# Down-projection weights loaded two neighbouring rows per partition, with the activations transposed by every second column

## The chip, the cores and the metric

The kernel runs on one core of one Trainium2 chip. The metric is the device time of one execution in microseconds (us). Three runs of the kernel before gave 1525.69, 1526.43 and 1526.97 us; the median is 1526.43 us.

## The reference, cut to what matters

The program is one decoder layer on 512 tokens of width 1024: a state-space mixer and a pooling mixer, a layer norm, a mixture of 32 experts of which every token uses 4, and a second layer norm. The change lies in the experts. One expert block, with its inputs `xb` (tokens by 1024) and the expert's number `e`, is

```python
g = xb @ w_gate[e] + b_gate[e]
u = xb @ w_up[e] + b_up[e]
g = jnp.minimum(g, SWIGLU_LIMIT)
u = jnp.clip(u, -SWIGLU_LIMIT, SWIGLU_LIMIT)
glu = g * jax.nn.sigmoid(SWIGLU_ALPHA * g)
return ((u + 1.0) * glu) @ w_down[e] + b_down[e]
```

All three weights of an expert are 1024 x 1024 float32, 4 MB each. The results of a token's four experts are added with the router's weights. All weights of all 32 experts (384 MB) are read from HBM once.

## The kernel before

A front part (the mixers, the first norm, the router, the gate of the per-layer inputs) fills the first 410 us. Then come the experts, one after the other in the fixed order `ORD`, and a short tail with the last norm. An expert has 64, 96 or 128 slots for tokens (`CAP`, only experts 2 and 3 have 128); its slots are worked on in blocks of 32 (`NB` = 4 blocks at most).

**Loads.** Every weight matrix is loaded in four quarters of 256 rows of the contraction, 1 MB each, into a ring of 16 buffers of 128 partitions x 2 x 1024 float32 (`raw_tile`, `RAWS`). `raw_load` (L1212 to L1216) issues them from SyncE in the order gate 0 to 3, up 0 to 3, down 0 to 3, and `do_load` issues the load 16 places ahead as soon as the matmuls of the present one are in the program. For gate and up, partition p of quarter q holds the rows 8p + 2q and 8p + 2q + 1, which are neighbours in HBM (8 KB in one piece, 32 KB from the piece of the next partition). For down, partition p holds the rows 256q + p and 256q + 128 + p (two pieces of 4 KB, 512 KB apart; the pieces of neighbouring partitions are neighbours in HBM).

**Matmuls.** `mm_tile` (L1117 to L1127) multiplies one quarter: for each block of 32 slots and each of the two rows of a partition, four matmuls of 32 stationary columns and 256 moving columns, one for each quarter of the output columns, which lie in four strips of 32 output partitions. Two instructions stand in the trace for each of them, so a quarter of an expert with 64 slots shows 32 instructions, with 96 slots 48, with 128 slots 64. The kernel's loop goes over positions i in `ORD`: in position i come gate and up of expert i, then down of expert i - 1.

**Between them.** The result of gate and up leaves `u2` with 32 x 4 partitions (strip j, slot) and, for block b, 256 columns; the element at strip j and column c is hidden unit 256j + c. `h_T` (L1138 to L1142) turns it over for the down matmuls by TensorE transposes of 128 x 128 (`u2` is the stationary operand, `ident` the moving one) and a copy on ScalarE into `ht`. A transpose takes 128 columns that lie next to each other: the first takes the columns 0 to 127 of the block, the second 128 to 255, which fits rows p and 128 + p of a quarter. `h_T_rows` (L1144 to L1151) does the same for the last expert, whose down matmuls go through `mm_rows`. Beside the weights, GpSimd issues for every position the indirect transfers that add the results to the output rows (L1160, four 256-column pieces at most) and gather the inputs of a later expert (L1016).

A loop for overflowing experts (at the end of the file) uses the same helpers.

Of the kernel before, what the change touches and what calls it, by code (L numbers as in the profile page):

```python
# [37 lines left out]
NB = 4  # L38
# [30 lines left out]
def _layer(top, tc, nc, x, xT, pT, ssm, ssm_d, log_step, w_in, w_val, w_glg, w_pg, pscale, w_pp,  # L69
# [5 lines left out]
    TE = nc.tensor  # L75
# [11 lines left out]
    def tps():  # L87
        return psum.tile([128, 512], F32, tag="tp", name="tp", bufs=2)
# [30 lines left out]
    ident = keep.tile([128, 128], F32, name="ident")  # L119
# [55 lines left out]
    def new():  # L175
        slot[0] += 1
        return sm[:, slot[0] - 1]
# [64 lines left out]
    kq, r = new(), new()  # L242
# [97 lines left out]
    for q4 in range(4):  # L340
        pt = tps()
# [248 lines left out]
    for slot in range(24):  # L590
# [4 lines left out]
        g_, n_ = ((up_g, 1) if slot < 4 else (gb_g, 1) if slot < 12 else (pp_g, 2) if slot < 16 else (ga_g, 1))  # L595
# [6 lines left out]
    for kk in range(4):  # L602
        pt = tps()
# [380 lines left out]
    def raw_tile(dt_=F32):  # L984
        pool, tag, bufs = ring[rn[0] % RAWS]
        rn[0] += 1
        return pool.tile([128, 2, D], dt_, tag=tag, name="eraw", bufs=bufs)
# [3 lines left out]
    for n in range(len(ring)):  # L991
        r = raw_tile()
# [145 lines left out]
    def h_T(u2, ht, g_, n_=2):  # L1138
        pt = tps()
        for i in range(2 * n_):  # L1140
            TE.transpose(pt[:, i * 128:(i + 1) * 128], u2[:, (4 * g_ + i) * 128:(4 * g_ + i + 1) * 128], ident)  # L1141
        S.copy(ht[:, 2 * g_:2 * g_ + n_], pt[:, :256 * n_].rearrange("p (b u c) -> p b u c", b=n_, u=2))  # L1142

    def h_T_rows(u2, ht, g_, n_):  # L1144
        pt = tps()
        for i in range(2 * n_):
            TE.transpose(pt[:, i * 128:(i + 1) * 128], u2[:, (4 * g_ + i) * 128:(4 * g_ + i + 1) * 128], ident)
        for i in range(n_):
            b = 2 * g_ + i
            S.copy(ht.rearrange("p (j u) c -> p u j c", u=2)[:, :, :, b * 32:(b + 1) * 32],  # L1150
                   pt[:, i * 256:(i + 1) * 256].rearrange("p (u j s) -> p u j s", u=2, j=4))  # L1151
# [16 lines left out]
    def g_min(pg, w_=512):  # L1168
        g_ = mz.tile([128, 512], F32, tag="g", name="g", bufs=2)
        ts(g_[:, :w_], pg[:, :w_], LIMIT, OP.min)  # L1170
        return g_
# [14 lines left out]
    def u2_tile():  # L1186
        return mz.tile([128, D], F32, tag="u2", name="u2", bufs=2)
# [23 lines left out]

    def raw_load(src, q_, down):  # L1212
        r = raw_tile()
        v = src.rearrange("(k p) c -> p k c", p=128) if down else src.rearrange("(p k) c -> p k c", k=8)
        nc.sync.dma_start(r, v[:, 2 * q_:2 * q_ + 2])
        return r  # L1216

    seq = []
# [9 lines left out]
    def do_load(n):  # L1228
        if n < len(seq) and n not in raws:
            i, m_, q_ = seq[n]  # L1230
            c = ORD[i - (m_ == 2)]
            w_ = (w_gate, w_up, w_down)[m_]
            if c < 2:
                src = w_[c]
            else:
                if c not in RG:
                    RG[c] = nc.sync.value_load(eid[0:1, c:c + 1], min_val=0, max_val=(E - 1) * D)
                src = w_.rearrange("e k c -> (e k) c")[bass.ds(RG[c], D), :]
            raws[n] = raw_load(src, q_, m_ == 2)
# [5 lines left out]
    def hooks(i, s):  # L1245
# [4 lines left out]
        if s == 0:  # L1250
            if p_ is not None:
                HT[p_] = h_tile() if i < E else x_tile()
                for g_ in banks(p_):
                    if i < E:
                        h_T(U2[p_], HT[p_], g_, min(2, nb_of(p_) - 2 * g_))
                    else:
                        h_T_rows(U2[p_], HT[p_], g_, min(2, nb_of(p_) - 2 * g_))
            if c is not None:
                PG[c], PU[c] = ([acc() for _ in banks(c)] for _ in range(2))
                if i > 0:  # L1260
                    bias(0, c)(PG[c])
                    bias(1, c)(PU[c])
            if nx is not None:
                X[nx] = x_tile()
                for q_ in range(2):
                    half_T(xgs[(i + 1) % 2], X[nx], q_, CAP[nx], (S.copy, V.tensor_copy)[q_])
                SL[nx] = sel_e(nx)
            if i + 2 < E:
                gather(xgs[i % 2], ls[:, ORD[i + 2]], CAP[ORD[i + 2]])
# [98 lines left out]
    with tc.manual_schedule():  # L1368
# [11 lines left out]
        for i in range(E + 1):  # L1380
            for s in range(12):
# [6 lines left out]
                if here:  # L1388
                    _, m_, q_ = seq[n]
                    w_ = raws.pop(n)  # L1390
                    if m_ == 2:
                        c = ORD[i - 1]
# [7 lines left out]
                    else:  # L1400
                        c = ORD[i]
# [27 lines left out]
    with tc.For_i(0, nb_, 1) as it:  # L1429
# [36 lines left out]
        for m_ in range(2):  # L1466
            os = [acc(), acc()]
            for q_ in range(4):
                mm_tile(os, xt_, raw_load(wv[m_], q_, False), q_, NB, pre=bias_v(m_))
            pp.append(os)  # L1470
        u2 = u2_tile()
        for n0 in range(2):
            g_ = g_min(pp[0][n0])
            tt(g_, g_, g_sig(g_), OP.mult)
            glu(u2, n0, u_clip(pp[1][n0]), g_)
        for g_ in range(2):
            h_T(u2, ht_, g_)
        os = [sacc(), sacc()]
        for q_ in range(4):
            mm_tile(os, ht_, raw_load(wv[2], q_, True), q_, NB, True, True)  # L1480
# [47 lines left out]
```

## Time and profile before

| | us |
|---|---|
| median of three runs | 1526.43 |
| the profiled execution | 1529.48 |
| its span, first to last instruction | 1527.8 |
| TensorE matmuls busy | 1359.0 (89%) |
| VectorE / GpSimd / ScalarE busy | 438.5 / 286.4 / 245.8 |
| bytes read from HBM | 453 MB |

Slices of the page show the DMA engines nearly idle for stretches of the front part and fully busy from about 420 us to about 1460 us, at 372 to 408 GB/s. A load is a DMA issued by SyncE ("SPq"); it is split over 16 DMA engines and has landed when the slowest of them is done. In a row of a timeline the first two numbers are the start and the length of a run of like instructions; "x32" is their count; the brackets hold the idle time ahead and what ended it.

### The profile page before, as it was taken

What the parts mean: (1) busy time and instruction counts of PE and PEld (TensorE: products, weight loads), DVE (VectorE), ACT (ScalarE), POOL (GpSimd) and SP (SyncE); (2) the same over time, 40 slices, a digit from 0 to 9 for tenths busy, and PEclk for the clock granted to TensorE, in tenths of its full rate; (3) what the DMA queues carried; (4) which work ended last, traced back from release to release, by engine and by line L of the source; (5) the groups of instructions that cost most, each with busy time, mean ns of one, the idle gap of its engine ahead of it and who ended that gap; (6) DMA issues with size and microseconds to landing.
All of it is one profiled execution on the core that took longest, in us unless ns stands there. A gap on an engine that the chain in (4) does not pass through costs nothing.

```text
span 1527.8 us, 41208 instructions
## 1 busy us (share of the span) xinstructions
PE 1359.0 (89%) x18454; PEld 876.3 (57%) x18454; DVE 438.5 (29%) x940; ACT 245.8 (16%) x436; POOL 286.4 (19%) x293
## 2 busy tenths in 40 slices
PE   6779999999699999997989889989898899799993
PEld 6658887767566665554545445545454455456651
DVE  3986747577311111110101011111110111111105
ACT  2434334242100010000100000000100000000011
POOL 0294310003401121111112111111121111110132
PEclk9889999999899999999999999999999999999997
DMA  4412325731699999999999999999999999999963
GB/s 154 134 53 72 99 86 194 222 116 46 219 401 389 398 389 372 390 397 394 393 388 387 386 377 384 392 388 395 383 393 382 381 381 395 391 384 405 408 210 139
DMA packets 124164, 468.58 MB, mean 307 GB/s; under 512 B 19757, under 2 KB 44785, under 8 KB 91216
## 3 DMA queue, kind: packets, MB, share of 16 engines
q1 hardware_dynamic: 107248, 446.12, 75.8%
q0 software_dynamic: 16736, 19.79, 6.0%
q8 instruction: 146, 2.39, 0.6%
q14 instruction: 34, 0.28, 0.1%
HBM read 453.23 MB, written 17.80 MB: 308 GB/s over the span
## 4 chain that ended last, share of the span: by engine, by line
DMA 48%; PE 39%; DVE 5%; issue 4%; POOL 3%; ACT 0%; SPq 0%; DVEq 0%; ACTq 0%; POOLq 0%
DMA eraw<-in_w_down_dram 22%; DMA eraw<-in_w_up_dram 14%; PE acc L1125 14%; PE ss L1125 9%; DMA eraw<-in_w_gate_dram 8%; PE acc L116 3%; PE acc L117 3%; PE acc L115 3%; DMA lsb<-in_log_step_dram 2%; POOL lst L817 1%; PE acc L1132 1%; PE tp L1141 1%; PE acc L1208 1%; PE tp L1009 1%; DMA raw<-in_w_out_dram 1%
## 5 line engine op out<-in xcount | busy, mean ns | idle before, releaser
L1125 PE MATMUL acc<-eraw,xt 128*32 128x256 f32 x10880 | 619.2, 386 | 67.8 <-DMA eraw<-in_w_up_dram 62.3
L1125 PEld LDWEIGHTS acc<-eraw,xt 128*32 128x32 f32 x10880 | 350.2, 111 | 324.5 <-DMA eraw<-in_w_up_dram 90.2
L1125 PE MATMUL ss<-eraw,ht 128*32 128x256 f32 x5312 | 298.3, 380 | 20.4 <-DMA eraw<-in_w_down_dram 20.4
L1160 POOL DMA_INDIRECT acc_d<-y,ix x83 | 129.6, 1561 | 880.2 <-ACT y L1194 864.3
L1125 PEld LDWEIGHTS ss<-eraw,ht 128*32 128x32 f32 x5312 | 171.5, 110 | 143.1 <-DMA eraw<-in_w_down_dram 33.7
L1142 ACT COPY ht<-tp 128x512 f32<-128x512 f32 (+1 forms) x50 | 23.9, 516 | 659.3 <-PE tp L1141 659.3
L183 DVE TENSOR_SCALAR u<-acc 128x512 f32<-128x512 f32 (+1 forms) x51 | 30.6, 600 | 301.9 <-PE acc L1125 293.3
L181 DVE TENSOR_SCALAR g<-acc 128x512 f32<-128x512 f32 (+1 forms) x51 | 30.7, 603 | 288.9 <-PE acc L1125 278.4
L1010 DVE COPY xt<-tp 128x384 f32<-128x384 f32 (+2 forms) x32 | 16.4, 512 | 312.4 <-PE tp L1009 312.3
L115 PE MATMUL acc<-ahi,hi 128*128 128x512 f32 x160 | 64.5, 403 | 15.2 <-DVE sm L191 15.2
L1175 ACT ACTIVATE s<-g 128x512 f32<-128x512 f32 (+1 forms) x51 | 27.9, 559 | 284.6 <-DVE g L181 284.6
L104 DVE TENSOR_TENSOR lo<-raw,hi 128x1024 fp32r<-128x1024 f32 (+1 forms) x52 | 63.1, 1216 | 28.2 <-ACT hi L103 27.8
L103 ACT CAST hi<-raw 128x1024 fp32r<-128x1024 f32 (+1 forms) x53 | 54.9, 1036 | 72.4 <-PE acc L116 48.8
L117 PE MATMUL acc<-ahi,lo 128*128 128x512 f32 x160 | 64.0, 400 | 0.0
L116 PE MATMUL acc<-alo,hi 128*128 128x512 f32 x160 | 63.7, 398 | 0.0
L115 PEld LDWEIGHTS acc<-ahi,hi 128*128 128x128 f32 x160 | 31.0, 194 | 21.7 <-ACT hi L103 15.5
L1016 POOL DMA_INDIRECT xg<-hd,ls x32 | 32.5, 1017 | 33.3 <-PE tp L1009 23.9
L116 PEld LDWEIGHTS acc<-alo,hi 128*128 128x128 f32 x160 | 31.0, 194 | 6.3
L117 PEld LDWEIGHTS acc<-ahi,lo 128*128 128x128 f32 x160 | 30.7, 192 | 6.6
L1194 ACT ACTIVATE y<-ss,ls 128x256 f32<-128x256 f32 x83 | 33.9, 482 | 0.0
L187 DVE TENSOR_TENSOR g<-g,s 128x512 f32<-128x512 f32 (+1 forms) x51 | 29.2, 601 | 13.1 <-ACT s L1175 13.1
L191 DVE SCALAR_TENSOR_TENSOR u<-u,g 128x512 f32<-128x512 f32 (+1 forms) x51 | 30.8, 603 | 1.7
(404 smaller groups left out, 1291.6 us busy)
## 6 DMA issues: line engine op xcount, KB each, us to landing
eraw<-in_w_gate_dram SPq DMA_DIRECT2D x128, 1024.0 KB
eraw<-in_w_up_dram SPq DMA_DIRECT2D x128, 1024.0 KB
eraw<-in_w_down_dram SPq DMA_DIRECT2D x128, 1024.0 KB
raw<-in_w_in_dram SPq DMA_DIRECT2D x23, 512.0 KB
raw<-in_w_out_dram SPq DMA_DIRECT2D x8, 512.0 KB
raw<-in_w_ple_gate_dram SPq DMA_DIRECT2D x8, 512.0 KB
raw<-in_w_pool_proj_dram SPq DMA_DIRECT2D x4, 512.0 KB
raw<-in_w_glu_val_dram SPq DMA_DIRECT2D x4, 512.0 KB
```

Source lines behind the costliest of these rows:

```text
L103: S.copy(h, v)
L104: (lo_eng or V).tensor_tensor(l, v, h.bitcast(F32), op=OP.subtract)
L115: TE.matmul(o, lhsT=lh, rhs=rh, start=start, stop=False)
L116: TE.matmul(o, lhsT=lh, rhs=rl, start=False, stop=False)
L117: TE.matmul(o, lhsT=ll, rhs=rh, start=False, stop=stop)
L181: V.tensor_scalar(o, i, a, None, op0=op)
L183: V.tensor_scalar(o, i, a, b, op0=op, op1=op1)
L191: V.scalar_tensor_tensor(o, a, s, b, op0=op0, op1=op1)
L1016: P.indirect_dma_start(out=xg[:n_], out_offset=None, in_=hd, in_offset=bass.IndirectOffsetOnAxis(ap=lst_[:n_, 0:1], axis=0), bounds_check= ...
L1125: TE.matmul(os[b // 2][j * 32:(j + 1) * 32, b % 2 * 256:b % 2 * 256 + 256], lhsT=x_, rhs=w_[:, kk, j * 256:(j + 1) * 256], start=first and ...
L1160: q_ = P.indirect_dma_start(out=acc_d.rearrange("t (j c) -> (t j) c", j=4), out_offset=bass.IndirectOffsetOnAxis(ap=ix_[b], axis=0), in_=y ...
L1194: S.activation(y_[:, b * 256:(b + 1) * 256], py[b // 2][:, c_], AF.Copy, scale=w_.bitcast(F32))
```

## The change

The loads of the down weights take quarter q as rows 256q + 2p and 256q + 2p + 1 in partition p: one piece of 8 KB per partition, and the pieces of neighbouring partitions are neighbours in HBM, so a load reads one stretch of 1 MB. For the products to stay the same, the transposes take every second column of a block: the first columns 0, 2, 4, ..., the second columns 1, 3, 5, .... The stationary operand is then read with a step of 8 bytes instead of 4. The numbers of loads, bytes, transposes, matmuls and copies stay what they were.

```diff
     def h_T(u2, ht, g_, n_=2):
         pt = tps()
         for i in range(2 * n_):
-            TE.transpose(pt[:, i * 128:(i + 1) * 128], u2[:, (4 * g_ + i) * 128:(4 * g_ + i + 1) * 128], ident)
+            TE.transpose(pt[:, i * 128:(i + 1) * 128], u2.rearrange("p (b c u) -> p b u c", b=NB, u=2)[:, 2 * g_ + i // 2, i % 2], ident)
         S.copy(ht[:, 2 * g_:2 * g_ + n_], pt[:, :256 * n_].rearrange("p (b u c) -> p b u c", b=n_, u=2))
 
     def h_T_rows(u2, ht, g_, n_):
         pt = tps()
         for i in range(2 * n_):
-            TE.transpose(pt[:, i * 128:(i + 1) * 128], u2[:, (4 * g_ + i) * 128:(4 * g_ + i + 1) * 128], ident)
+            TE.transpose(pt[:, i * 128:(i + 1) * 128], u2.rearrange("p (b c u) -> p b u c", b=NB, u=2)[:, 2 * g_ + i // 2, i % 2], ident)
...
     def raw_load(src, q_, down):
         r = raw_tile()
-        v = src.rearrange("(k p) c -> p k c", p=128) if down else src.rearrange("(p k) c -> p k c", k=8)
-        nc.sync.dma_start(r, v[:, 2 * q_:2 * q_ + 2])
+        if down:
+            nc.sync.dma_start(r, src[q_ * 256:(q_ + 1) * 256].rearrange("(p k) c -> p k c", k=2))
+        else:
+            nc.sync.dma_start(r, src.rearrange("(p k) c -> p k c", k=8)[:, 2 * q_:2 * q_ + 2])
         return r
```

## Rows read from the trace of the kernel before

**Rows 1.** Windows: PE, PEld, DVE, ACT, POOL busy, clock, DMA share, GB/s.

```profile
410.00:590.00 180.00, 177.41 (x3115) 110.29 (x3117) 30.29 (x57) 17.61 (x38) 27.14 (x22) 1.00 1.02 389
598.00:1374.00 776.00, 688.02 (x11618) 395.85 (x11608) 97.61 (x188) 66.44 (x149) 114.13 (x82) 0.98 1.02 387
1374.00:1502.00 128.00, 127.07 (x1926) 71.71 (x1927) 20.18 (x37) 14.23 (x31) 20.70 (x14) 1.00 0.88 333
```

**Rows 2.** Waits of PE from 598 to 1374 us: us in total, times, longest.

```profile
PE acc L1125 <- DMA eraw<-in_w_up_dram: 62.3, 44, 2.9
PE ss L1125 <- DMA eraw<-in_w_down_dram: 19.8, 35, 1.3
```

**Rows 3.** Timeline of PE, from its last wait for a load on.

```profile
1374.19 1.93 PE L1125 MATMUL ss<-eraw,ht 128*32 128x256 f32 x32 [0.61 <-DMA eraw<-in_w_down_dram]
1376.06 0.87 PE L1141 MATMUL tp<-ident,u 128*128 128x128 f32 x6
...
1378.46 27.83 PE L1125 MATMUL acc<-eraw,xt 128*32 128x256 f32 x512
...
1416.58 1.09 PE L1141 MATMUL tp<-ident,u 128*128 128x128 f32 x8
...
1453.63 0.87 PE L1141 MATMUL tp<-ident,u 128*128 128x128 f32 x6
...
1479.21 0.66 PE L1147 MATMUL tp<-ident,u 128*128 128x128 f32 x4
```

**Rows 4.** Waits of SyncE's queue from 598 to 1374 us.

```profile
SPq L1215 <- DMA eraw<-in_w_down_dram: 176.9, 91, 2.4
SPq L1215 <- DMA eraw<-in_w_gate_dram: 164.6, 86, 3.4
SPq L1215 <- PE acc L1125: 154.5, 69, 7.0
```

**Rows 5.** Chain that ended last, from 620 us: start, us, what.

```profile
620.98 25.26 DMA eraw<-in_w_up_dram
...
646.36 20.09 DMA eraw<-in_w_gate_dram
...
666.57 23.25 DMA eraw<-in_w_down_dram
```

**Rows 6.** Timeline of SyncE's queue, groups of four issues, 700 to 1380 us.

```profile
718.13 7.70 SPq L1215 DMA_DIRECT2D eraw<-in_w_up_dram  x4
727.95 7.85 SPq L1215 DMA_DIRECT2D eraw<-in_w_down_dram  x4
...
1026.37 7.96 SPq L1215 DMA_DIRECT2D eraw<-in_w_up_dram  x4
...
1343.43 7.86 SPq L1215 DMA_DIRECT2D eraw<-in_w_down_dram  x4
...
1366.29 8.31 SPq L1215 DMA_DIRECT2D eraw<-in_w_up_dram  x4
```

**Rows 7.** Tile eraw, 1000 to 1100 us: one issue on SyncE, ns min/median/max.

```profile
L1215 SPq DMA_DIRECT2D eraw<-in_w_down_dram x12: 373/383/4147, 1002.1 to 1078.2; - x12
...
L1215 SPq DMA_DIRECT2D eraw<-in_w_up_dram x11: 332/333/333, 1026.4 to 1099.5; - x11
```

**Rows 8.** Windows of the first experts, each with loads of one kind.

```profile
456.00:464.00 8.00, 8.00 (x156) 4.82 (x152) 2.15 (x4) 0.00 (x0) 0.00 (x0) 1.00 1.01 415
438.00:442.00 4.00, 4.00 (x68) 2.56 (x70) 0.56 (x2) 0.59 (x2) 0.95 (x1) 1.00 1.02 421
471.00:476.00 5.00, 5.00 (x76) 3.12 (x78) 0.82 (x2) 2.55 (x6) 2.12 (x2) 1.00 1.02 409
```

**Rows 9.** Line 1141, all transposes: weight loads, ns min/median/max.

```profile
L1141 PEld LDWEIGHTS tp<-ident,u x166: 138/140/145, 436.5 to 1454.1; 128*128 128x128 f32 x166
```

**Rows 10.** Line 115, 5 to 60 us: weight loads with every fourth column, then adjacent ones.

```profile
L115 PEld LDWEIGHTS acc<-hi,ahi x32: 307/310/334, 5.2 to 30.3; 128*128 128x128 f32 x32
...
L115 PEld LDWEIGHTS acc<-ahi,hi x13: 187/188/330, 46.6 to 59.7; 128*128 128x128 f32 x13
```

## The prediction

> **What bounds the kernel now.** I read the windows first, stage by stage, since the page's 89% of TensorE busy mixes stages. From 410 us to 1374 us the DMA engines are busy without a gap (share 1.02, 387 to 389 GB/s), while TensorE is busy in 688.02 of the 776 us from 598 on [rows 1]. What ended TensorE's idle time there is, in the list of waits, always a weight load: 62.3 us for up and 19.8 us for down [rows 2]. The last such wait ends at 1374.19 us, before the last down quarter of a 64-slot expert; from there TensorE runs almost without a gap (127.07 of 128 us), and loads arrive ahead of it [rows 1, 3]. So the time is: the moment at which that load lands, plus 154 us (1527.8 - 1374.2) of work that TensorE sets. A faster load moves the first part; a slower transpose adds to the second.
>
> Who sets the landing? SyncE's queue waits mostly for landings (176.9 us for down, 164.6 us for gate), and the chain that ended last runs over loads alone: up, gate, down, each issued when the one before landed [rows 4, 5]. In the order gate 0 to 3, up 0 to 3, down 0 to 3 these three stand eight places apart: a load goes out when the one eight places earlier has landed, and so eight loads are under way at any time. 20 to 25 us for eight loads is 2.5 to 3.2 us for one. SyncE also waits 154.5 us for TensorE to free buffers, 7.0 us at most [rows 4]; with eight loads (20 us) queued this doesn't drain the DMA engines. The stretch is thus a sum of landings, one behind the other, and every down load in it counts in full.
>
> How many are there? After 1374 us follow 512 instructions of gate and up, two matrices of four quarters with 64 each [rows 3]: a 128-slot expert. Experts 2 and 3 are the only ones, and this late in `ORD` it is expert 3, position 29. The down quarter at 1374.19 is that of position 27, the 28th expert: 28 x 4 = 112 down loads, all issued after 410 us.
>
> **The change, part by part.** *The loads.* The price of a landing can be read from the issues. The four up loads of an expert are issued as the four down loads eight places before them land, and the four down loads as gate loads land. A group of four issues spans three such landings and its last issue's own duration. Between 700 and 1380 us there are 20 groups of up issues; 14 of them took 7.91 to 7.97 us, five 7.60 to 7.73, one 8.31, with a mean of 7.90. Of the down groups ten were held by nothing else, at 7.81 to 7.88 us, mean 7.86; the rest, above 10 us, also waited for buffers [rows 6]. (The group of rows holds the first and the last of either kind and one of the usual up groups.) An up issue lasts 0.333 us, a down issue 0.38 [rows 7]. So a down load (4 KB pieces) lands (7.96 - 0.333) / 3 = 2.54 us after the one before, a gate load (8 KB pieces, same bytes, same buffers) (7.86 - 0.38) / 3 = 2.493 us. The difference is 0.047 us; with the mean of all 20 groups (7.90) it is 0.030 us. After the change a down load has the pieces of a gate load. I take 0.047 us, the usual group, since the five short ones fall where another DMA engine was the last: 112 x 0.047 = 5.3 us. The low end is 112 x 0.030 = 3.4 us.
>
> The early windows check this from another side. There the 16 engines are still in step, so a window holds loads of one kind: gate and up at 415 GB/s (456 to 464 us), down at 421 (438 to 442 us) and 409 (471 to 476 us) [rows 8]. A megabyte (1.0486 MB) at 415 takes 2.527 us, at 409 2.564 us; this difference is 0.037 us, and the first down window shows none at all. The high end pairs the slowest of these with the best: 2.564 less 2.491 (at 421) is 0.073 us, 8.2 us for 112. Below zero is a rival of its own.
>
> The skill weighs on this as follows. The Trainium skill, "DMA: Bandwidth & Descriptors", section Specifications, gives 512 bytes as the size from which a transfer runs at line rate; both 4 KB and 8 KB pieces are beyond it, and by that rule the sum would be zero, which is the second rival below. The same page, section "Why small descriptors are slow (HBM only)", has a fixed cost of about three cycles for a packet beside one cycle for each 32 bytes; by it two packets of 4 KB cost 262 cycles and one of 8 KB 259, and an estimate of the sum from this would be 1.1% of 2.54 us, 3.2 us for 112.
>
> *The issues.* A down issue should last 0.333 us like an up issue, instead of 0.38 [rows 7]; SyncE waits between issues, so this is worth nothing. The number of bytes, buffers and landings waited for is unchanged.
>
> *The transposes.* 170 transposes (166 in `h_T`, four in `h_T_rows`) read their stationary operand with a step of 8 bytes. A weight load of adjacent columns takes 140 ns there [rows 9]. The trace has none with a step of 8 bytes; the nearest row is the first matmul stage, which takes every fourth column (16 bytes) as stationary: 310 ns against 188 ns for adjacent columns [rows 10]. So the price of one lies between 0 and 122 ns. Before 1374 us even the upper price hides: at most 166 - 20 = 146 transposes there make 17.8 us [rows 3, 9], against 82.1 us that TensorE idles for loads [rows 2]. After 1374 us nothing hides it: 6 + 8 + 6 + 4 = 24 transposes [rows 3] now go at one per 0.14 us (0.87 / 6), the pace of their weight loads, so they would cost up to 24 x 0.122 = 2.9 us. I take zero: half the step of the row, and half of it would still be only 1.5 us; the range keeps 2.9.
>
> The Trainium skill, "SBUF — State Buffer", section Specifications, says that the memory has lines of 16 bytes and that two hits in a line are enough for the full rate; a step of 8 bytes gives two float32 a line, a step of 16 bytes one. By that rule the cost is zero, and the row of the 16-byte step agrees with its other half.
>
> *Sum.* 5.3 us less. The profiled execution took 1529.48 us (span 1527.8, with 1.7 us around it), 3.05 us above the median of 1526.43; 1529.48 - 5.3 = 1524.2 for it, and for the median 1521.1. TensorE can follow: at 1333 us and at every earlier wait the landings come earlier by nearly as much, and the 82.1 us of its idle time are far more than 5.3.
>
> **The rivals.** *A larger gain.* If all down landings go from the slowest early rate to the best one, 8.2 us come off, 1518.2; if in addition the 19.8 us that TensorE waits for down loads [rows 2] shrank by half, some 10 us, 1516. Against it: the usual groups show 0.047 us.
>
> *Nothing moves.* If the 2.54 us of a down load come from which DMA engine is last, and not from the size of its pieces, the time stays at 1526.4. The early window of down loads at 421 GB/s [rows 8] and the five short groups speak for it; the 14 groups at 7.91 to 7.97 against ten at 7.81 to 7.88, which don't overlap, against. A load that is still cut into 4 KB pieces would give the same time; gate loads, of the same form, have 8 KB pieces.
>
> *The gain is eaten by the transposes.* At 122 ns each the end takes 2.9 us more: 1526.43 - 5.3 + 2.9 = 1524.0.
>
> *Slower.* One load would now read a single stretch of 1 MB from HBM by 16 DMA engines, where gate loads spread their pieces 32 KB apart over 4 MB. If such a stretch is served worse, as when transfers crowd each other, the nearest rate is the mean of the long stretch with its scatters and gathers, 387 GB/s [rows 1], 2.71 us for a load: 112 x 0.17 = 19 us more, 1545. It decides from 0.027 us a load on (3.05 / 112). Against it: the down loads of before read two such stretches of 512 KB and reach 409 to 421 GB/s [rows 8].
>
> **How the numbers follow.** Forecast 1521.1 us, chance 0.52, its own range 1518 to 1523. Larger gain 0.15, nothing moves 0.14, eaten by the transposes 0.11, slower 0.08. A measurement of this kernel can tell about 0.2%, 3.05 us, from no change. The larger gain and nearly all of the forecast (its low end is 3.4 us) are faster by more: 0.15 + 0.48 = 0.63. The rest of the forecast, the two middle rivals: 0.04 + 0.14 + 0.11 = 0.29 the same. Slower 0.08. The range goes from 1515 (all of the larger gain) to 1527.5 (nothing moves, with a part of the transposes' cost), and leaves out the slower rival and little beside it.
>
> **What would show it.** In the profile after, the 128 down loads should show 128 packets of 8 KB each in place of 256 of 4 KB, so 32768 packets fewer under 8 KB. A group of up issues should last about (3 x 2.493) + 0.333 = 7.81 us instead of 7.96: at 7.96 the first step is wrong. The last wait of TensorE for a load should end near 1369 us and the work behind it still take 154 us; if that has grown, the transposes did it, and weight loads of line 1141 above 140 ns say by how much. Copies on ScalarE and matmuls should last as long as before. The prediction is wrong if the landings of up loads, which now share the engines with 8 KB pieces when GpSimd's transfers come in, grow by what the down loads give.

## The result, and the profile after

The changed kernel took 1517.43 us (median of 4 runs, 1515.33 to 1518.69) where the kernel before took 1526.7 us beside it: a ratio of 0.9939, with a 95% interval of 0.9925 to 0.9953. It is 9.3 us faster; the forecast was 5.3 us. The direction and the range (1515 to 1527.5) held, the size did not: 1517.43 lies just outside the forecast's own range of 1518 to 1523, where the rival of a larger gain had been put. The profiled execution took 1518.69 us (span 1517.0) against 1529.48 (span 1527.8).

The page's line on the DMA engines (packets in all, bytes, mean rate, packets under three sizes), kernel after:

```profile
DMA packets 107780, 468.58 MB, mean 309 GB/s; under 512 B 19757, under 2 KB 44785, under 8 KB 58448
```

The same line of the kernel before has 124164 packets and 91216 under 8 KB, with the same bytes. So the change did what it says: 91216 - 58448 = 32768 packets fewer under 8 KB.

Windows of the kernel after, columns as in [rows 1]:

```profile
410.00:590.00 180.00, 177.50 (x3082) 108.01 (x3084) 30.08 (x57) 17.41 (x38) 26.92 (x21) 0.99 1.02 393
598.00:1374.00 776.00, 696.74 (x11824) 405.93 (x11816) 98.40 (x192) 68.84 (x156) 118.52 (x84) 0.99 1.02 393
```

The DMA share is still 1.02, so the stretch is still full, but the rate rose from 389 and 387 GB/s [rows 1] to 393. TensorE is busy 8.7 us more in the long stretch, as more of its work fits in.

Waits of TensorE for weight loads from 598 to 1374 us, kernel after (total, times, longest), which answer to [rows 2]:

```profile
PE acc L1125 <- DMA eraw<-in_w_up_dram: 45.4, 36, 2.9
PE ss L1125 <- DMA eraw<-in_w_down_dram: 31.4, 42, 2.1
```

The waits for up fell from 62.3 to 45.4 us; those for down rose from 19.8 to 31.4. The sum fell by 5.3 us. Who waits for which load shifted with the phase of the work; a load that lands faster is not always the one that TensorE waits less for.

Timeline of TensorE from its last wait for a load on, kernel after, which answers to [rows 3]:

```profile
1363.01 1.93 PE L1125 MATMUL ss<-eraw,ht 128*32 128x256 f32 x32 [0.56 <-DMA eraw<-in_w_down_dram]
1364.88 0.99 PE L1141 MATMUL tp<-ident,u 128*128 128x128 f32 x6
...
1405.52 1.22 PE L1141 MATMUL tp<-ident,u 128*128 128x128 f32 x8
...
1442.67 0.98 PE L1141 MATMUL tp<-ident,u 128*128 128x128 f32 x6
...
1468.37 0.74 PE L1147 MATMUL tp<-ident,u 128*128 128x128 f32 x4
```

The last wait ends at 1363.01 us instead of 1374.19 (the forecast was near 1369), and 1517.0 - 1363.0 = 154.0 us follow instead of 153.6. The whole gain came before the last landing, none behind it; the question is thus why the landings gave about 10 us and not 5.

### The profile page after: what moved, and what is told of

The parts are those of the page before. It is cut to its first block, busy times and chain, and to the rows that moved or that the text cites. A ratio compares the mean times of both kernels' runs of the same rounds, so it can differ in the third digit from the quotient of the medians.

```text
span 1517.0 us, 41208 instructions
## 1 busy us (share of the span) xinstructions
PE 1356.2 (89%) x18454; PEld 877.0 (58%) x18454; DVE 438.2 (29%) x940; ACT 245.5 (16%) x436; POOL 287.7 (19%) x293
## 2 busy tenths in 40 slices
DMA packets 107780, 468.58 MB, mean 309 GB/s; under 512 B 19757, under 2 KB 44785, under 8 KB 58448
## 3 DMA queue, kind: packets, MB, share of 16 engines
HBM read 453.23 MB, written 17.80 MB: 311 GB/s over the span
## 4 chain that ended last, share of the span: by engine, by line
DMA 56%; PE 30%; DVE 5%; issue 4%; POOL 3%; ACT 0%; SPq 0%; DVEq 0%; ACTq 0%; POOLq 0%
DMA eraw<-in_w_down_dram 23%; DMA eraw<-in_w_up_dram 15%; DMA eraw<-in_w_gate_dram 14%; PE acc L1125 10%; PE ss L1125 5%; PE acc L116 3%; PE acc L117 3%; PE acc L115 3%; DMA lsb<-in_log_step_dram 2%; POOL lst L817 1%; PE acc L1132 1%; PE tp L1141 1%; DMA raw<-in_w_out_dram 1%; DMA lst<-dfl 1%; DVE eraw L191 1%
## 5 line engine op out<-in xcount | busy, mean ns | idle before, releaser
L1125 PE MATMUL acc<-eraw,xt 128*32 128x256 f32 x10880 | 608.7, 382 | 47.8 <-DMA eraw<-in_w_up_dram 45.4
L1125 PE MATMUL ss<-eraw,ht 128*32 128x256 f32 x5312 | 303.1, 383 | 31.4 <-DMA eraw<-in_w_down_dram 31.4
L1125 PEld LDWEIGHTS ss<-eraw,ht 128*32 128x32 f32 x5312 | 171.5, 111 | 158.6 <-DMA eraw<-in_w_down_dram 45.2
L115 PEld LDWEIGHTS acc<-ahi,hi 128*128 128x128 f32 x160 | 31.0, 194 | 21.6 <-ACT hi L103 15.4
```

The source lines that it names most:

```text
L115: TE.matmul(o, lhsT=lh, rhs=rh, start=start, stop=False)
L1125: TE.matmul(os[b // 2][j * 32:(j + 1) * 32, b % 2 * 256:b % 2 * 256 + 256], lhsT=x_, rhs=w_[:, kk, j * 256:(j + 1) * 256], start=first and ...
```

## The experiments

Each was timed in five rounds beside the kernel before, which took 1526.93 us beside the first four kernels, 1526.14 beside the next four and 1528.88 beside the last four. Two questions were open. Does the gain come from the size of the pieces, or from the order in which the addresses are read? And was the price of an undisturbed load too low, or do loads that meet other transfers gain more than others?

**The loads without the transposes.** The kernel after with its old transposes:

```diff
-TE.transpose(..., u2.rearrange("p (b c u) -> p b u c", b=NB, u=2)[:, 2 * g_ + i // 2, i % 2], ident)
+TE.transpose(..., u2[:, (4 * g_ + i) * 128:(4 * g_ + i + 1) * 128], ident)
```

> The down loads of the kernel after (8 KB pieces, one stretch of 1 MB) with the transposes of the kernel before (columns next to each other); rows and columns no longer belong together, so the down product is another one. If the loads carry the whole gain: 1517 us, 9 to 10 us under the kernel before, and transposes back at 140 ns a weight load, 0.4 us better than the kernel after. If the every-second-column transposes had a share in the gain: clearly above 1517 us.

Measured: 1516.43 us, ratio 0.9933 (0.9917 to 0.9949), 10.5 us faster than the kernel before. The loads carry the whole gain.

**The transposes without the loads.** The kernel before with the opposite edit:

```diff
-TE.transpose(..., u2[:, (4 * g_ + i) * 128:(4 * g_ + i + 1) * 128], ident)
+TE.transpose(..., u2.rearrange("p (b c u) -> p b u c", b=NB, u=2)[:, 2 * g_ + i // 2, i % 2], ident)
```

> The loads of the kernel before (4 KB pieces) with the transposes of the kernel after (every second column); the down product is another one. If the step of 8 bytes costs 69 ns a weight load (209 against 140 ns) and most of it hides behind the matmuls: before + 0.4 us, 1527 us, no difference that can be told. If the 24 transposes behind the last load cost the full 69 ns: before + 1.7 us. If the transposes had a share in the gain: under 1524 us.

Measured: 1527.09 us, ratio 0.9998 (0.9988 to 1.0009): no change that can be told. The weight loads of line 1141 (ns min/median/max) in this kernel, and then in the one with the new loads alone:

```profile
L1141 PEld LDWEIGHTS tp<-ident,u x166: 194/209/221, 435.1 to 1452.1; 128*128 128x128 f32 x166
```

```profile
L1141 PEld LDWEIGHTS tp<-ident,u x166: 137/140/145, 433.7 to 1441.3; 128*128 128x128 f32 x166
```

A step of 8 bytes makes a weight load 69 ns longer (209 against 140), and yet the time doesn't show it.

**Pieces of 8 KB, 32 KB apart.** The down weights are loaded as gate and up are:

```diff
-nc.sync.dma_start(r, src[q_ * 256:(q_ + 1) * 256].rearrange("(p k) c -> p k c", k=2))
+nc.sync.dma_start(r, src.rearrange("(p k) c -> p k c", k=8)[:, 2 * q_:2 * q_ + 2])
```

> As the kernel after, but a down load takes its pieces of 8 KB as gate and up do, 32 KB apart over 4 MB instead of one stretch of 1 MB; the rows of the down weights are then others than the hidden units, so the product is another one. If the size of the pieces makes the gain: as the kernel after, 1517 us. If the single stretch of 1 MB makes it: as before, 1526 us. If half and half: 1522 us.

Measured: 1515.91 us, ratio 0.9928 (0.9913 to 0.9942), 11.0 us faster than the kernel before.

**Pieces of 4 KB in one stretch of 1 MB.** The kernel after with 32 bytes between the two rows of a buffer, so that a piece cannot span them:

```diff
-    def raw_tile(dt_=F32):
+    def raw_tile(dt_=F32, pad=False):
...
-        return pool.tile([128, 2, D], dt_, tag=tag, name="eraw", bufs=bufs)
+        t_ = pool.tile([128, 2 * D + 8], dt_, tag=tag, name="eraw", bufs=bufs)
+        if pad:
+            return t_.rearrange("p (k c) -> p k c", k=2)[:, :, :D]
+        return t_[:, :2 * D].rearrange("p (k c) -> p k c", k=2)
...
-        r = raw_tile()
+        r = raw_tile(pad=down)
```

> As the kernel after, same rows in the same partitions and the same stretch of 1 MB, but the two rows of a partition stand 32 bytes apart in the buffer, so that each goes as a piece of 4 KB; buffers are 32 bytes longer. The result is the layer's. If the size of the pieces makes the gain: as before plus the transposes, 1526 to 1527 us, and up issues go out 7.95 us a group of four again. If the single stretch makes it: 1517 us.

Measured: 1530.01 us, ratio 1.0019 (1.001 to 1.0029), 3.1 us slower than the kernel before. Its page shows the pieces back at the count of before:

```profile
DMA packets 124164, 468.58 MB, mean 306 GB/s; under 512 B 19757, under 2 KB 44785, under 8 KB 91216
```

In this kernel the groups of four up issues last 7.86 to 7.98 us, all 20 from 700 to 1380 us, as with the 4 KB pieces of before [rows 6].

These four settle the first question. With 8 KB pieces the time is 1515.9 to 1517.4 us in either order of addresses, with 4 KB pieces 1526.9 to 1530.0 in either order. The one stretch of 1 MB gives nothing by itself. (The last kernel is slower than the 1526 to 1527 us that were expected of it; its 3.1 us may come from the one stretch or from the offset of 32 bytes, which wasn't separated.)

**Half of the weight matmuls.** To see the landings without TensorE behind them, both kernels were run with one of the two rows of a partition multiplied:

```diff
-            for kk in range(2):
+            for kk in range(1):
...
-                              stop=q_ == 3 and kk == 1, skip_group_check=True)
+                              stop=q_ == 3, skip_group_check=True)
```

> The kernel before with half of the matmuls of every weight quarter left out (the second row of each partition), so that TensorE is never the bound and the loads set the end of all 32 experts. This is the base for the next run; the loads and GpSimd's transfers stay. Expected 50 to 100 us below the kernel before, since the matmuls behind the last load shrink.

> The kernel after with the same half of the matmuls left out; 128 down loads count now instead of 112. If a 4 KB pair costs 0.083 us a load more than 8 KB pieces wherever it lies: 10 to 11 us under the half-PE base. If TensorE's share in the bound had hidden a part of the gain: more than 12 us. If 0.047 us a load is the whole price and the rest of the gain came from TensorE's schedule: 6 us.

Measured: 1507.82 us for the kernel before so cut (ratio 0.9881, 0.9863 to 0.9898), 1497.06 for the kernel after (0.9809, 0.9791 to 0.9826). The first is 18 us under the kernel before and not the 50 to 100 that were expected: the loads of all 32 experts now set the end, and TensorE's last wait for one ends at 1451.55 us of a span of 1501.7. The gain of the change is 10.8 us, as large as with all matmuls. So TensorE neither makes nor eats it: it lies in the transfers.

**The same without GpSimd's transfers.** In addition, the gathers of the expert loop and its scatters are left out:

```diff
-            if i + 2 < E:
-                gather(xgs[i % 2], ls[:, ORD[i + 2]], CAP[ORD[i + 2]])
...
-            scatter4(YT.pop(pp), [ix4[:, b, pp:pp + 1] for b in range(nb_of(pp))])
+            YT.pop(pp)
```

> As the half-PE base, and GpSimd's transfers between the experts are left out too (the scatters of the results of 31 experts and the gathers of 30), so that only the weights run on the DMA engines. Base for the next run. The time falls below the half-PE base by what those transfers cost the landings, 20 us or more.

> The kernel after with the same parts left out. If the price of the smaller pieces is that of an undisturbed landing, as read from the issues (0.047 us): 128 x 0.047 = 6 us under its base, and the other 4 us of the gain come from stretches in which GpSimd's transfers run beside the loads. If every piece has a fixed price of about 0.01 us on its engine, disturbed or not: 10 us under its base, as with the transfers.

Measured: 1403.06 us (0.9193, 0.9177 to 0.9209) and 1397.21 (0.9153, 0.9137 to 0.9169). Without GpSimd's transfers the kernel before is 105 us faster, far more than the 20 or more that were expected. The gain of the change is 5.85 us, 0.046 us for each of the 128 down loads. Windows of the first and then of the second of these kernels:

```profile
600.00:1000.00 400.00, 267.11 (x3494) 126.32 (x3492) 56.23 (x112) 39.69 (x92) 0.00 (x0) 0.88 1.02 419
```

```profile
600.00:1000.00 400.00, 266.60 (x3500) 125.27 (x3492) 56.77 (x112) 38.84 (x89) 0.00 (x0) 0.89 1.01 422
```

A load of 1.0486 MB takes 2.503 us at 419 GB/s and 2.485 at 422; three loads of which one is for down differ by 0.053 us. Both figures are near the price of the prediction, 0.047 us, once nothing else moves. The rest of the gain is there only when GpSimd's transfers run.

**Gathers issued for all 128 partitions.** Which of GpSimd's transfers? In the trace of before, a gather for 96 slots stands at 1011.56 us, one for 128 slots at 1281.82. Windows some 7 us behind each:

```profile
1018.00:1022.00 4.00, 1.93 (x32) 0.94 (x32) 0.00 (x0) 0.00 (x0) 0.00 (x0) 1.00 1.04 279
1289.00:1292.00 3.00, 3.00 (x62) 1.80 (x58) 0.32 (x1) 0.00 (x0) 0.00 (x0) 1.00 1.01 413
```

Behind the small gather the DMA engines are as busy (1.04) and move a third less; behind the large one they don't slow. So the last four kernels issue every gather for 128 partitions; the added slots hold an index out of bounds and bring no token:

```diff
 def gather(xg, lst_, n_=128):
+    n_ = 128
```

Two of them have half of the weight matmuls, two are otherwise the whole kernels.

> The half-PE kernel before, but every gather of GpSimd is issued for all 128 partitions instead of the 64 or 96 slots of the expert (the slots beyond hold no token and move nothing). The one gather of 128 slots in the traces (at 1281 us in the kernel before) leaves the loads at 413 GB/s, one of 96 slots at 1011 us pushes them to 279 GB/s. If the number of partitions makes this: 20 us or more below the half-PE base of 1507.8 us. If it was chance: 1507 us.

> The half-PE kernel after with the same gathers. If the part of the gain beyond 0.047 us a load came from the stretches that the gathers slow down: 6 us under the run before this one. If it came from the scatters or lies in every load: 10 to 11 us under it.

> The whole kernel before with gathers issued for all 128 partitions; the result is the layer's. If the gathers of 64 and 96 slots slow the loads: 15 to 60 us below before, and TensorE's waits for up loads (62 us before) mostly gone. If not: 1526 us.

> The whole kernel after with gathers issued for all 128 partitions; the result is the layer's. If loads still set the end: 5 to 6 us (112 x 0.047) under the run before this one. If TensorE has become the bound: the same time as that run within 2 us, and the change of this case is worth nothing on top.

Measured, with half of the matmuls: 1481.6 us (0.97, 0.9683 to 0.9718) and 1475.49 (0.966, 0.9639 to 0.968), a gain of 6.1 us. Measured, whole: 1500.78 us (0.9824, 0.9807 to 0.9841) and 1494.45 (0.9789, 0.9769 to 0.9808), a gain of 6.3 us. One expectation failed: TensorE's waits for up loads in the whole kernel before, 62.3 us, didn't mostly go but fell to 45.2. With these gathers the gain is that of the kernels without GpSimd's transfers, though the scatters run. And the last kernel is 34 us faster than the kernel before beside it and about 23 us faster than the changed one: the better version of both.

## Why the prediction was right, and where its size failed

**What bounds the kernel** held: a full stretch of landings, then 154 us of TensorE's work. That the gain stayed at 10.8 us with half of the weight matmuls shows that the landings set it.

**The price of an undisturbed load** held. Three pairs of runs give 5.85 and 6.1 us for 128 loads (128 x 0.047 = 6.0) and 6.3 us for 112, where the sum was 112 x 0.047 = 5.3. That bears out the choice of 0.047 over the mean's 0.030; no run shows the reason given for it, another DMA engine that was the last in the five short groups. The calm groups of up issues show the price too; SyncE's timeline of the kernel after:

```profile
747.75 7.81 SPq L1217 DMA_DIRECT2D eraw<-in_w_up_dram  x4
815.11 7.81 SPq L1217 DMA_DIRECT2D eraw<-in_w_up_dram  x4
...
1018.29 7.81 SPq L1217 DMA_DIRECT2D eraw<-in_w_up_dram  x4
...
1051.21 9.37 SPq L1217 DMA_DIRECT2D eraw<-in_w_up_dram  x4
```

Eleven of the 20 groups from 700 to 1380 us last 7.78 to 7.82 us, the number that was forecast, against 7.96 in [rows 6]. The other nine last from 8.5 to 10.0 us, and with them the mean of the 20 is 8.44 us, above the 7.90 of before. So the test that the prediction set holds in the calm groups alone. What fell is the time of a whole expert: over 23 of them, from the gathers at 574.13 and 575.73 us on, one gather follows the other after 33.84 us in the mean before and after 33.30 now. Why nine groups are longer isn't shown; either kind begins 11 to 17 us behind a gather.

**The step that failed is the term of the sum that priced all 112 loads alike.** The price was read from groups of issues that nothing held up, and the down groups above 10 us were set aside as waiting for buffers [rows 6]. But in every expert a part of the loads lands while a gather of 64 or 96 slots is under way, and the change gained 9.3 to 11.0 us with such gathers against 5.85 to 6.3 without them. The windows from 6 to 12 us behind four gathers in a row, kernel before (gathers at 737.05, 767.70, 806.32 and 836.88 us) and then kernel after (732.53, 763.88, 800.70 and 831.25):

```profile
743.05:749.05 6.00, 5.86 (x112) 3.25 (x100) 0.00 (x0) 0.00 (x0) 0.00 (x0) 1.00 1.02 323
773.70:779.70 6.00, 3.10 (x56) 1.61 (x52) 0.69 (x1) 0.10 (x1) 0.00 (x0) 0.98 1.02 305
812.32:818.32 6.00, 6.00 (x118) 3.41 (x109) 0.00 (x0) 0.00 (x0) 0.00 (x0) 1.00 1.02 325
842.88:848.88 6.00, 3.96 (x64) 1.93 (x62) 0.00 (x0) 0.00 (x0) 0.00 (x0) 0.91 1.03 319
```

```profile
738.53:744.53 6.00, 5.86 (x112) 3.25 (x100) 0.00 (x0) 0.00 (x0) 0.00 (x0) 1.00 1.04 336
769.88:775.88 6.00, 2.06 (x40) 1.02 (x40) 0.00 (x0) 0.00 (x0) 0.00 (x0) 0.95 1.05 353
806.70:812.70 6.00, 6.00 (x116) 3.41 (x108) 0.00 (x0) 0.00 (x0) 0.00 (x0) 1.00 1.03 349
837.25:843.25 6.00, 2.13 (x36) 0.94 (x32) 0.00 (x0) 0.00 (x0) 0.00 (x0) 1.00 1.04 343
```

The four rates of before average 318 GB/s, those of after 345; over all gathers from 574 us to 1345 us (23 and 24 of them) the means are 325 and 349. From 14 to 32 us behind a gather the rates are 418 and 413. This doesn't say that the change gains nothing there, as the pair without GpSimd's transfers rose from 419 to 422: a window doesn't hold the same loads before and after. Over the 32 us from a gather on, about one expert, the mean rose from 387.4 to 392.2 GB/s, by 1.24%. With gathers for 128 partitions the same windows of 32 us give 398.1 and 401.3, 0.80%. Over the 785 us or so of this stretch, 1.24% makes 9.7 us and 0.80% makes 6.3 us: the two sizes of the gain.

Which loads meet the gathers can be counted in the trace's records of single packets on SyncE's queue. In the kernel before, of the weight packets that start 6 to 12 us behind one of the 23 gathers, 7611 have 4 KB and 1142 have 8 KB, so three quarters of the bytes belong to down loads; from 14 to 32 us it is 5093 and 17791, an eighth. Two packets of 4 KB took 407 ns in the mean in the first stretch and one of 8 KB 382; in the second 325 and 314. So it is mostly down loads that meet a gather, and the disadvantage of small pieces more than doubles there. As packets overlap (a DMA share of 1.02), these records say where the surplus lies, but not how many us it makes.

How sure is this? Four comparisons with the gathers as they were gave 9.3, 10.5, 11.0 and 10.8 us; three without small gathers gave 5.85, 6.1 and 6.3. The two sets don't meet, though a single comparison is uncertain by some 2 to 4 us. That about 4 of the 10 us hang on the small gathers is shown by taking them away. Why a piece of 4 KB suffers more beside one is not shown; no run tried that. Nor do the windows place the 4 us finely: with large gathers too, the 6 us from 6 us on rise (from 395 to 413 GB/s, mean of 24), and those from 14 us on fall (from 415 to 406).

**The rivals.** A larger gain had the size (1516 to 1518.2) but not the mechanism: it wanted undisturbed landings to gain 0.073 us, where the runs show 0.046 to 0.056, and fewer waits of TensorE for down, which grew. Its lower time was also added up wrongly: 8.2 us and half of 19.8 make 18 us, or 1508, and not 1516. So that the measured time lies in the stated range is in part luck: the forecast's own range ended at 1518, and the rest down to 1515 was kept for this rival. That nothing moves is out, as pieces of 8 KB instead of 4 KB were worth 0.046 us a load even with no transfer of GpSimd's about. The Trainium skill, "DMA: Bandwidth & Descriptors", section Specifications, puts full rate at 512 bytes and above; by that rule nothing would have moved, and these runs don't agree with it. The estimate from the same page of the Trainium skill, section "Why small descriptors are slow (HBM only)", was 3.2 us for 112 loads, between half and two thirds of what the three pairs measured. The slower rival, one stretch of 1 MB served worse, is out at its size of 19 us: with 8 KB pieces one stretch (1517.43) and pieces 32 KB apart (1515.91) differ by 1.5 us, with intervals that overlap.

**The transposes** were taken at zero between bounds of 0 and 122 ns. They cost 69 ns a weight load, in the middle of the bounds. By the rule of the Trainium skill, "SBUF — State Buffer", section Specifications, that two hits in a line of 16 bytes are enough for the full rate, a step of 8 bytes would have been free; this weight load doesn't agree with it. That the transposes alone took no time that can be told (1527.09 against 1526.93 us) fits the reason that was given, that before the last wait TensorE's idle time covers them: 146 x 0.069 makes 10 us against 82.1. Behind that wait the four runs of 6, 8, 6 and 4 take 0.99, 1.22, 0.98 and 0.74 us for 0.87, 1.09, 0.87 and 0.66 in [rows 3], 0.44 us in all, which is the growth from 153.6 to 154.0, and not 24 x 0.069 = 1.7: the pace there, 0.16 us for one, is less than the 0.209 of a weight load, so these overlap.

**The issues** were costed at nothing, and the reading beside them was wrong. SyncE's waits of 154.5 us for TensorE [rows 4] were taken for buffers that TensorE had not freed. After the change, with the same buffers and more TensorE work, SyncE's waits from 598 to 1374 us are:

```profile
SPq L1217 <- DMA eraw<-in_w_up_dram: 228.9, 90, 4.3
SPq L1217 <- DMA eraw<-in_w_down_dram: 199.1, 92, 3.6
SPq L1215 <- DMA eraw<-in_w_gate_dram: 172.2, 88, 3.5
SPq L1217 <- PE acc L1125: 4.2, 15, 0.4
```

150 us of "PE acc" are gone, and the three kinds of landing now share nearly all of the waits. With half of the weight matmuls, where TensorE is done sooner, the same entry is still 137.3 us with the loads of before and 1.3 us with those of after. So buffers that TensorE held did not hold SyncE in the kernel before. The entry lies where SyncE's issue instructions are long: from 1012.1 to 1019.9 us, where one issue of a gate load takes 7.4 us, it makes 6.2 us. The down groups above 10 us are long for the same reason in part (one issue of a down load took 4.1 us [rows 7]); the last section has more.

## What to carry to other kernels

Where a stretch is a row of landings, double the piece if the layout allows it, even from 4 KB to 8 KB: it was worth about 2% of each load in clear water, and nearly twice as much in all, as loads beside the small gathers gained more. Price a load from all of its landings, the disturbed ones included, and look at the rate just behind each small transfer of another queue before calling the long groups something else's wait. If that rate drops while the DMA share stays full, change the shape of the small transfer first: here that was worth more than the change under study.

## What the hardware showed that was not expected

**Indirect gathers of 64 or 96 partitions slow the transfers beside them; the same gathers issued for 128 do so far less.** The two windows above show 279 against 413 GB/s with the DMA engines busy throughout; from 6 to 12 us behind a gather the means over all gathers are 325 and 395 GB/s with the loads of before, 349 and 413 with those of after. Issuing all of them for 128 partitions took 26.2 us (1507.82 to 1481.6) and 21.6 us (1497.06 to 1475.49) off the kernels with half of the matmuls, and 28 and 23 us off the whole ones. This holds although more is read, not less: the whole kernel before reads 453.23 MB from HBM with the small gathers, and with the large ones, by its page,

```profile
HBM read 458.86 MB, written 17.80 MB: 319 GB/s over the span
```

The 5.6 MB are 4 KB for each of 1376 added slots. Why the small gathers slow the rest isn't shown. GpSimd's own row for such a gather, in the faster whole kernel, and the windows 6 us behind this and the next gather (at 1052.35 us):

```profile
1021.65 1.07 POOL L1017 DMA_INDIRECT xg<-hd,ls  x1 [0.30 <-issue]
```

```profile
1027.65:1033.65 6.00, 6.00 (x120) 3.62 (x112) 0.00 (x0) 0.00 (x0) 0.00 (x0) 1.00 1.02 417
1058.35:1064.35 6.00, 2.94 (x56) 1.44 (x52) 0.00 (x0) 0.00 (x0) 0.00 (x0) 1.00 1.04 417
```

**Pieces of 4 KB made SyncE's issue instructions long.** Issues of gate loads, which follow four down loads, in the stretch from 1000 to 1100 us (ns min/median/max), in the kernel before and then in the kernel after:

```profile
L1215 SPq DMA_DIRECT2D eraw<-in_w_gate_dram x12: 333/1090/7695, 1012.2 to 1091.9; - x12
```

```profile
L1217 SPq DMA_DIRECT2D eraw<-in_w_gate_dram x12: 332/333/337, 1005.1 to 1083.6; - x12
```

An issue took up to 7.7 us with four loads of 256 pieces ahead of it, and never above 0.337 us from 598 us on in the kernel after, with loads of 128 pieces alone. The kernel before with half of the matmuls and without GpSimd's transfers has the long ones too (median 998, longest 4674 ns from 598 us on), and its gain was 5.85 us: the long issues do not by themselves make the surplus of 4 us. Whether they make a part of the 0.046 us is open, as every kernel with 4 KB pieces had both.
